# Seven products instead of eight in the down projection of three groups, with weight sums made by adding DMAs

## The chip, the cores and the metric

The kernel runs on one core of a Trainium2 chip. The core has a matrix engine (TensorE, PE in the rows, with its weight loads as PEld), a vector engine (VectorE, DVE), a scalar engine (ScalarE, ACT), GpSimd (POOL) and a queue engine (SyncE, SP) from which most transfers are started. The metric is the device time of one execution in microseconds (us), smaller is better; the time before is the median of three runs.

## The reference

One layer of a decoder trunk on x of 512 tokens by 1024, in float32:

```python
h = rmsnorm(x, g1)
p = h @ w_in                      # attention 6x64, SSD 6 heads, pooling
x = x + concat(moba(p), ssd(p), pool(p)) @ w_out
h2 = rmsnorm(x, norm_ffn)
g, u = h2 @ w_gate, h2 @ w_up     # hidden width 2816
x = x + (silu(g) * u) @ w_down    # 2816 -> 1024
out = rmsnorm(x, norm_final)
```

The change lies in the last matrix product, `(silu(g) * u) @ w_down`, and in the preparation of the gate and up weights.

## The kernel before

**Products.** Every float32 product is made of three matmuls (`mm3`, L188 to L190): each operand is split into a rounded part `hi` (written by ACT, L881) and the rest `lo` (written by DVE, L882), and hi·hi, lo·hi and hi·lo are summed in a PSUM bank (128 x 512 floats). TensorE writes PSUM; DVE and ACT read it.

**The feed-forward part** begins at about 190 us in the trace and ends with the kernel. The hidden width is cut into 22 tiles of 128 (`FT`), in six groups: `GROUPS = ((0,4), (4,8), (8,12), (12,16), (16,18), (18,22))`. For each tile but tile 0 the gate and up projections together are made in seven half-size products (a Strassen form with sums of weights), numbered 1 to 7, each of 12 matmuls with 256 columns, 84 for a tile (`block`). Their results lie in three banks of the tile, psA, psB and psC; `block_out` (L1123 to L1146) copies or adds them to `g`, `ur` and `a`, with one short instruction of ACT or DVE behind each product. The tile's result `a` (128 x 512, silu(g)·u transposed) is split into `aTh` and `aTl`.

**The down projection of a group** comes after its tiles. For each half h of the 1024 output columns, for each tile k and for each of the four token tiles t, three matmuls of 512 columns add into `pd<group><h>_<t>`: 2 x 4 x 4 x 3 = 96 matmuls for a group of four tiles. After a half, four adds (`add_x1`, L814) put the four banks onto the residual `x1`. The weights are split into `dh` and `dl`, 128 x 1024 each, four pairs for a group.

**Preparation of weights.** Every weight tile is loaded from HBM by SP into one of four buffers (`NRAW`): `r_g`, `r_u` and `r_d`, 512 KB each. The `plan` is a list of stages: `split_g`, `add_up` (four adds of 512 columns on DVE, L931 to L934, that form the weight sums `sa` and `sb`), `split_v`, two of `split_s`, and `split_d`. Each stage takes places in a ring of 8 tiles (`w`) or 10 tiles (`wx`), and `done` gives them back when a product has used them. `advance` starts the next stage after each product where the ring has room and the planner's clock says that the load has landed; `need` forces it. The order of the products on TensorE is written by `pair_order`, and a static scheduler then fixes the order of each engine's instructions. Each engine works through its own list in order; an instruction that waits holds up all behind it on that engine.

Of the kernel before, what the change touches and what calls it, by code (L numbers as in the profile page):

```python
# [26 lines left out]
P = 128  # L27
S = 512
# [9 lines left out]
NRAW = 4  # L38
PLAIN = (0,)
# [77 lines left out]
def layer(tc, xT, xn, w1, wz, wv, wo, wgu, wd, par, poolw, gffn, gfin, out):  # L117
# [3 lines left out]
    with ctx:  # L121
# [685 lines left out]
        sp = fpool("sums", 2)  # L807
# [60 lines left out]

        ops = {}
# [14 lines left out]
        def all_loads():  # L884
            for lo_, hi_ in GROUPS:
                order = [(w, i) for i in range(lo_, hi_) for w in "gu"]
                if lo_ == 0:
                    first = [(w, i) for i in PLAIN for w in "gu"] + [("g", i) for i in EARLY]
                    order = first + [q for q in order if q not in first]
                for w, i in order:  # L890
                    yield (w, i), wgu[2 * i + (w == "u")]
                for h in range(2):
                    for kp in range(lo_ // 2, hi_ // 2):
                        yield ("d", kp, h), wd[2 * kp + h]

        loads = all_loads()
# [4 lines left out]

        def load_ahead():
            while len(raws) < NRAW:
                key, src = next(loads, (None, None))
                if key is None:
                    return
                raws[key] = rawp.tile([P, 1024], F32, name="r_" + "_".join(map(str, key)), tag="raw")
                nc.sync.dma_start(raws[key], src)
                dma_free[0] = max(dma_free[0], L.clock) + 1.6
                landed[key] = dma_free[0] + 2.5  # L910
# [6 lines left out]
        sums = {}  # L917

# [7 lines left out]
        def add_up(i):  # L926
            load_ahead()
            r0, r1 = raws["g", i], raws["u", i]
            g1, g2, v1, v2 = r0[:, :512], r0[:, 512:], r1[:, :512], r1[:, 512:]
            s_, q_ = sums[i] = [sp.tile([P, 1024], F32, name=f"{n}{i}", tag="s") for n in ("sa", "sb")]  # L930
# [4 lines left out]
            used(("g", i))  # L935

# [27 lines left out]
        plan = []  # L964
        for gi, (lo_, hi_) in enumerate(GROUPS):
            for i in range(lo_, hi_):
                stages = [("wx", 2, split_g, i), ("w", 0, add_up, i), ("wx", 1, split_v, i), ("wx", 2, split_s, i, 0), ("w", 2, split_s, i, 1)]
                if i in PLAIN:
                    stages = [("wx", 2, split_plain, i, "g"), ("wx", 2, split_plain, i, "u")]
                    if i == PLAIN[-1]:  # L970
                        stages += [("wx", 2, split_g, k) for k in EARLY]
                elif i in EARLY:
                    stages = stages[1:]
                plan += stages
            for h in range(2):
                for kp in range(lo_ // 2, hi_ // 2):
                    plan.append(("w", 2, split_d, kp, h))
# [4 lines left out]
        def advance(must=False):  # L982

            if not plan or live[plan[-1][0]] + plan[-1][1] > cap[plan[-1][0]]:
                return False
            load_ahead()
            _, _, f, *a = plan[-1]
            key = (a[1], a[0]) if f is split_plain else (takes.get(f.__name__), *a)
            if not must and key[0] and L.clock < landed.get(key, 1e9):
# [126 lines left out]
        aT = {}  # L1116
        gf = [None]
# [7 lines left out]
        def block_out(i, n, e):  # L1125
            gl, gr, ur = slice(0, 256), slice(256, 512), slice(256, 512)
            if n in (1, 6, 7):
                u_ = e["u1" if n == 1 else "u2" if n == 6 else "u3"] = (fw if n == 1 else ap_).tile(
                    [P, 256], F32, name=f"u{n}_{i}", tag=f"u{n}", bufs=len(EARLY) + 1 if n == 1 else 2
                )  # L1130
                nc.scalar.copy(u_, e["B"])  # L1131
            elif n == 2:
                e["g"] = fw.tile([P, S], F32, name=f"g{i}", tag="g", bufs=4)
                add(e["g"][:, gl], e["A"], e["u1"])
                nc.scalar.activation(e["g"][:, gl], e["g"][:, gl], AF.Silu)
            elif n == 4:
                e["a"] = e.get("a") or ap_.tile([P, S], F32, name=f"a{i}", tag="a")
                nc.vector.scalar_tensor_tensor(e["a"][:, :256], e["B"], -1.0, e["g"][:, gl], ALU.mult, ALU.mult)
            elif n == 3:
                add(e["g"][:, gr], e["C"], e["u2"])  # L1140
                last = nc.scalar.activation(e["g"][:, gr], e["g"][:, gr], AF.Silu)
                if i == FT - 1:

                    with tc.issue_after(last.ins):
                        nc.scalar.activation(tiny.tile([P, NT], F32, name="pre2", tag="pre"), rstd, AF.Sqrt)
                nc.vector.scalar_tensor_tensor(e["a"][:, ur], e["ur"], -1.0, e["g"][:, gr], ALU.mult, ALU.mult)  # L1146
                out_aT(i, e["a"])
                st.pop(i)
            if n in (5, 7) and "u3" in e and "C" in e:
                e["ur"] = ap_.tile([P, 256], F32, name=f"ur{i}", tag="ur")  # L1150
                add(e["ur"], e["C"], e["u3"])

        def block(i, n):
# [3 lines left out]
            e = st.setdefault(i, {})  # L1157
            which = {1: "B", 6: "B", 7: "B", 4: "B", 2: "A", 5: "C", 3: "C"}[n]
# [46 lines left out]
        def pair_order(lo_, hi_):


            tiles = [i for i in range(lo_, hi_) if i not in PLAIN]
            order = []
            for i, nxt in zip(tiles, tiles[1:] + [None]):  # L1210
                if (i, 6) not in order:
                    order += [(i, n) for n in (1, 2, 6, 5, 7) if (i, n) not in order and (i, n) not in FIRST and (n > 2 or i not in st)]
                if nxt is None and hi_ == 18:

                    return order + [(hi_, 1), (i, 4), (hi_, 2), (i, 3)], []
                if nxt is None:
                    return order, [(i, 4), (i, 3)]
                if nxt in EARLY:
                    order += [(nxt, 6), (i, 4), (nxt, 5), (i, 3), (nxt, 7)]
                else:  # L1220
                    order += [(nxt, 1), (i, 4), (nxt, 2), (i, 3)]

        for gi, (lo_, hi_) in enumerate(GROUPS):
# [91 lines left out]
def pack(inputs):  # L1315
# [23 lines left out]
    wgu = np.ascontiguousarray(wg).reshape(2 * FT, P, 1024)  # L1339
    wdn = f["w_down"][0].reshape(FT // 2, 2, P, 2, 512).transpose(0, 3, 2, 1, 4)  # L1340
# [15 lines left out]
    for g in range(4):  # L1356
# [3 lines left out]
        xT=xT, xn=x.reshape(NT, P, D), w1=w1, wz=wz, wv=wv, wo=wo, wgu=wgu, wd=wdn, par=par, poolw=poolw,  # L1360
# [19 lines left out]
```

## Time and profile before

| | before |
|---|---|
| median of 3 runs | 566.23 us (565.95 to 566.3) |
| profiled execution | 566.83 us, its span 565.0 us, granted clock 0.997 |
| TensorE busy | 555.0 us, 98% of the span |
| VectorE busy | 432.9 us, 77% |
| ScalarE busy | 305.4 us, 54% |
| GpSimd busy | 24.9 us, 4% |
| bytes moved | 61.61 MB, mean 109 GB/s |

The profiled execution is one execution with the hardware profiler on; its span is the time from its first to its last recorded instruction. Busy shares are averages over stages; what bounds a stage is read from that stage alone.

### The profile page before, as it was taken

How to read it: one execution, taken by the hardware profiler on the slowest of the kernel's cores; microseconds unless marked ns; L12 is line 12 of the kernel's file. 1: busy time of each engine (PE TensorE's matmuls, PEld its weight loads, DVE VectorE, ACT ScalarE, POOL GpSimd, SP SyncE). 2: the span in 40 equal slices, each digit the busy share in tenths (PEclk: the TensorE clock that was granted, in tenths of full speed). 3: DMA queues.
4: the chain of work that ended last, by engine and by line, in shares of the span. 5: the costliest groups of instructions: out<-in, count | busy, mean ns of one | idle time of the engine just before them, and what ended most of it. 6: DMA issues, size and time to landing. Idle time of an engine off the chain costs nothing.

```text
span 565.0 us, 9054 instructions
## 1 busy us (share of the span) xinstructions
PE 555.0 (98%) x3500; PEld 502.2 (89%) x3500; DVE 432.9 (77%) x793; ACT 305.4 (54%) x562; POOL 24.9 (4%) x43
## 2 busy tenths in 40 slices
PE   8999999999999999999999999999999999999994
PEld 4998998888978889998899989998999889999984
DVE  5489766898998678999977776876877876876456
ACT  6676635777678447655365525543354525434344
POOL 2020002006110000000000000000000000000000
PEclk9999999999999999999999999999999999999998
DMA  8852232423114501355242232334043333212003
GB/s 279 297 182 76 75 127 98 131 77 103 65 39 148 224 2 37 102 170 177 74 148 93 99 111 75 115 118 142 29 156 83 108 111 113 87 64 75 1 1 148
DMA packets 19807, 61.61 MB, mean 109 GB/s; under 512 B 2333, under 2 KB 4021, under 8 KB 19765
## 3 DMA queue, kind: packets, MB, share of 16 engines
q1 hardware_dynamic: 19188, 60.00, 31.8%
q10 hardware_dynamic: 576, 1.05, 0.5%
q8 instruction: 27, 0.44, 0.3%
q14 instruction: 16, 0.12, 0.1%
HBM read 58.93 MB, written 2.11 MB: 108 GB/s over the span
## 4 chain that ended last, share of the span: by engine, by line
PE 85%; DVE 8%; ACT 2%; DMA 2%; issue 1%; SPq 1%; DVEq 0%; ACTq 0%
PE psB L188 7%; PE psB L190 7%; PE psB L189 7%; PE pd L188 6%; PE pd L189 6%; PE pd L190 6%; PE pc L188 4%; PE pc L190 4%; PE pc L189 4%; PE psC L190 3%; PE psC L189 3%; PE psC L188 3%; PE po L188 2%; PE po L189 2%; PE po L190 2%; PE pn L188 2%
## 5 line engine op out<-in xcount | busy, mean ns | idle before, releaser
L189 PE MATMUL pd<-dl,aTh 128*128 128x512 f32 x160 | 62.4, 390 | 0.0
L188 PE MATMUL pd<-dh,aTh 128*128 128x512 f32 x160 | 61.4, 391 | 0.0
L190 PE MATMUL pd<-dh,aTl 128*128 128x512 f32 x160 | 59.1, 390 | 0.0
L158 DVE TENSOR_TENSOR wlo<-raw,whi 128x1024 fp32r<-128x1024 f32 (+4 forms) x35 | 37.2, 1066 | 12.7 <-ACT whi L157 12.7
L157 ACT ACTIVATE whi<-raw 128x1024 fp32r<-128x1024 f32 (+4 forms) x36 | 32.0, 892 | 21.2 <-PE pc L189 11.5
L881 ACT ACTIVATE sh<-sb 128x1024 fp32r<-128x1024 f32 x21 | 22.3, 1060 | 36.9 <-PE pd L189 15.5
L1131 ACT COPY u<-psB 128x256 f32<-128x256 f32 x63 | 23.2, 368 | 34.7 <-PE psB L190 34.0
L188 PE MATMUL pc<-hT_hi,whi 128*128 128x512 f32 x104 | 41.7, 401 | 0.0
L190 PE MATMUL pc<-hT_hi,wlo 128*128 128x512 f32 x104 | 40.8, 392 | 0.0
L189 PE MATMUL pc<-hT_lo,whi 128*128 128x512 f32 x104 | 40.7, 391 | 0.0
L882 DVE TENSOR_TENSOR gl<-r_g,gh 128x1024 fp32r<-128x1024 f32 x22 | 26.9, 1224 | 15.1 <-ACT gh L881 10.6
L881 ACT ACTIVATE dh<-r_d 128x1024 fp32r<-128x1024 f32 x22 | 23.3, 1058 | 24.0 <-PE psC L189 11.6
L881 ACT ACTIVATE gh<-r_g 128x1024 fp32r<-128x1024 f32 x22 | 23.3, 1058 | 23.0 <-DMA r_g<-wgu 12.8
L188 PEld LDWEIGHTS pd<-dh,aTh 128*128 128x128 f32 x160 | 30.0, 188 | 6.2 <-ACT aTh L881 0.4
L190 PEld LDWEIGHTS pd<-dh,aTl 128*128 128x128 f32 x160 | 29.9, 188 | 6.1
L189 PEld LDWEIGHTS pd<-dl,aTh 128*128 128x128 f32 x160 | 30.1, 188 | 5.8
L814 DVE TENSOR_TENSOR x<-pd,x 128x512 f32<-128x512 f32 x44 | 27.9, 686 | 8.1 <-PE pd L190 8.1
L882 DVE TENSOR_TENSOR sl<-sa,sh 128x1024 fp32r<-128x1024 f32 x21 | 25.7, 1224 | 8.8 <-PE psA L189 8.2
L882 DVE TENSOR_TENSOR sl<-sb,sh 128x1024 fp32r<-128x1024 f32 x21 | 25.6, 1221 | 8.0 <-ACT sh L881 8.0
L881 ACT ACTIVATE sh<-sa 128x1024 fp32r<-128x1024 f32 x21 | 22.3, 1062 | 14.6 <-DVE sa L932 9.0
L882 DVE TENSOR_TENSOR dl<-r_d,dh 128x1024 fp32r<-128x1024 f32 x22 | 26.9, 1222 | 4.1 <-ACT dh L881 4.0
L188 PE MATMUL po<-whi,mixT_hi 128*128 128x512 f32 x64 | 25.4, 400 | 0.0
(322 smaller groups left out, 1827.1 us busy)
## 6 DMA issues: line engine op xcount, KB each, us to landing
r_g<-wgu SPq DMA_DIRECT2D x22, 512.0 KB, 3.3
r_u<-wgu SPq DMA_DIRECT2D x22, 512.0 KB, 3.6
r_d<-wd SPq DMA_DIRECT2D x22, 512.0 KB, 3.4
raw<-w SPq DMA_DIRECT2D x13, 512.0 KB, 3.3
raw<-wo SPq DMA_DIRECT2D x8, 512.0 KB, 3.2
rawn<-xn SPq DMA_DIRECT2D x4, 512.0 KB, 5.8
x<-xn SPq DMA_DIRECT2D x4, 512.0 KB, 7.3
raw<-wz SPq DMA_DIRECT2D x4, 390.0 KB, 3.8
```

Of the source, the lines that this page charges most:

```text
L157: high = nc.scalar.activation(hi[:, sl], raw[:, sl], AF.Copy)
L158: eng.tensor_tensor(lo[:, sl], raw[:, sl], hi[:, sl].bitcast(F32), ALU.subtract)
L188: nc.tensor.matmul(ps, s_hi, m_hi, start=first, stop=False, skip_group_check=chain)
L189: nc.tensor.matmul(ps, s_hi, m_lo, start=False, stop=False, skip_group_check=chain)
L190: last_mm = nc.tensor.matmul(ps, s_lo, m_hi, start=False, stop=last, skip_group_check=chain)
L814: nc.vector.tensor_tensor(x1[t][:, cs], ps, x1[t][:, cs], ALU.add)
L881: high[name] = nc.scalar.activation(hi, src, AF.Copy).ins
L882: eng.tensor_tensor(lo, src, hi.bitcast(F32), ALU.subtract)
L1131: nc.scalar.copy(u_, e["B"])
```

## The change

For groups 1, 2 and 3 (`FAST`, tiles 4 to 15) the down projection is made in seven products in place of eight. The group's four tiles are two pairs `kp`; of each pair the 256 hidden rows by 512 tokens are one operand, cut into 2 x 2 blocks, and the weight (256 by 1024) the other. Seven sums of weight blocks R1 to R7 (`split_r`, 128 x 1024 with both pairs side by side) are multiplied with seven sums of blocks of `a` (`out_fast`, parts a1 to a7). One step (`down_step`) is one product for one pair: two token tiles of three matmuls of 512 columns, 6 matmuls. Seven products for two pairs make 84 matmuls for a group. Products 1, 6, 7, 4 chain in the banks `dnB0` and `dnB1`, products 2, 3, 5 in `dnA0` and `dnA1`; after the second pair of each product two adds put its banks onto `x1`: 14 adds for a group.

The steps don't stand behind the group: `MERGED` writes them between the products of the next group's first two tiles (n0, n1) and the last two products of the group's last tile (nl).

From tile 4 on (`ADD_FROM`) two of a tile's four weight sums are made by transfers: SP loads one array into a buffer, and a second transfer, started by GpSimd, adds another array to it (`sum_ahead`). The same forms two of the seven R. The new input `wgs` holds copies of blocks of `wgu` in another order. The up weights' load is half as large from there on. Buffers change: three for sums in place of two (one sum `R7` of a group lies in the buffer of `gn`), three in place of four for `u1` and for `g`. From tile 4 on, product 5 goes into the second half of psA's bank, and `ur` lies in the second half of psB's bank.

```diff
+FAST = (1, 2, 3)
+MERGED = (
+    "n0.1 1a nl.4 n0.2 1b nl.3 2a n0.5 6a n0.6 2b n0.7 6b n1.1 n0.4 5a n1.2 5b n0.3 7a n1.5 7b n1.6 3a n1.7 3b 4a 4b"
+).split()
...
-        sp = fpool("sums", 2)
+        sp = fpool("sums", SUM_BUFS)
...
+                    for sl, src in wd_block(key[1], *first):
+                        nc.sync.dma_start(t_[:, sl], src)
+                    for sl, src in wd_block(key[1], *second):
+                        nc.gpsimd.dma_start(t_[:, sl], src, accum_op=ALU.add)
+                else:
+                    nc.sync.dma_start(t_, wgs[2 * key[0]])
+                    nc.gpsimd.dma_start(t_, wgs[2 * key[0] + 1], accum_op=ALU.add)
...
+            if i >= ADD_FROM:
+
+                nc.vector.tensor_tensor(g1, sums[i, 0][:, :512], g1, ALU.add)
+                nc.vector.tensor_tensor(g2, g1, g2, ALU.add)
...
+        def split_r(kp, n):
+            load_ahead()
+            h_, l_ = (slot(R_RING[n - 1], f"r{x_}{kp}_{n}") for x_ in "hl")
...
+            if n == 6:
+
+                nc.vector.tensor_tensor(raws[r00], sums["r", kp, 5], raws[r00], ALU.add)
+                nc.vector.tensor_tensor(raws[r10], raws[r00], raws[r10], ALU.add)
...
-                e[which] = bank(f"ps{which}_{i}")[:, :256]
+                if which == "C" and i >= ADD_FROM:
+                    b_ = e["ac"][:, 256:]
...
-                e["ur"] = ap_.tile([P, 256], F32, name=f"ur{i}", tag="ur")
+                e["ur"] = e["bank"][:, 256:]
...
+        def out_fast(i, a_):
...
+            if j == 0:
+                half[kp] = a_
+                aT[1, kp] = part("a1", a_[:, L_])
+                nc.vector.tensor_tensor(a_[:, L_], a_[:, L_], a_[:, R_], ALU.subtract)
+                aT[5, kp] = part("a5", a_[:, L_], q)
+                return
+            a0 = half.pop(kp)
+            h_, l_ = part("a2", a_)
...
+            nc.vector.tensor_tensor(a0[:, R_], a_[:, R_], a0[:, R_], ALU.subtract)
+            sub(a_[:, R_], a0[:, L_], a_[:, R_])
+            sub(a_[:, L_], a_[:, R_], a_[:, L_])
+            h_, l_ = part("a4", a_)
...
+            aT[7, kp] = part("a7", a0[:, R_], q + 1)
...
+        def down_step(_, gi, n, c):
...
+            a_hi, a_lo = aT[n, kp0 + c]
+            new = n in (1, 2, 5)
+            for v in range(2):
+                vs = slice(v * P, (v + 1) * P)
+                mm3(ps[v], a_hi[:, vs], a_lo[:, vs], w_hi[:, js], w_lo[:, js], new and c == 0, c == 1, chain=not new)
+            if c:
...
+                    t0, h, op = {1: (0, 0, 0), 2: (0, 0, 0), 6: (2, 0, 0), 3: (2, 0, 0), 7: (2, 1, 1), 5: (2, 1, 1), 4: (0, 1, 1)}[n]
+                    cs = slice(h * 512, (h + 1) * 512)
+                    for v in range(2):
+                        x_ = x1[t0 + v][:, cs]
+                        if op:
+                            nc.vector.tensor_tensor(x_, x_, ps[v], ALU.subtract)
+                        else:
+                            add(x_, ps[v], x_)
```

TensorE at the start of group 1's down projection, before: psB_7 is the last product of tile 7, `pd10_0` and `pd10_1` are the first two token tiles of the group's half 0, `dh20` and `aTh4` the split weights and the split result of tile 4.

```order
L188 MATMUL psB_7_3437<-T3h_2329,sh17_3359 128x256
L189 MATMUL psB_7_3437<-T3l_2330,sh17_3359 128x256
L190 MATMUL psB_7_3437<-T3h_2329,sl17_3360 128x256
L188 MATMUL pd10_0_3550<-dh20_3382,aTh4_3246 128x512
L189 MATMUL pd10_0_3550<-dl20_3383,aTh4_3246 128x512
L190 MATMUL pd10_0_3550<-dh20_3382,aTl4_3247 128x512
L188 MATMUL pd10_1_3551<-dh20_3382,aTh4_3246 128x512
L189 MATMUL pd10_1_3551<-dl20_3383,aTh4_3246 128x512
L190 MATMUL pd10_1_3551<-dh20_3382,aTl4_3247 128x512
```

The same place after: psB_8 is product 1 of the next group's tile 8, `dnB0` and `dnB1` the two banks of step 1a, with `rh2_1` (R1) and the part `a1` of pair 2.

```order
L199 MATMUL psB_8_3580<-h2_hi_2077,gh8_3400 128x256
L200 MATMUL psB_8_3580<-h2_lo_2078,gh8_3400 128x256
L201 MATMUL psB_8_3580<-h2_hi_2077,gl8_3401 128x256
L199 MATMUL dnB0_1_3603<-rh2_1_3445,a1h2_3254 128x512
L200 MATMUL dnB0_1_3603<-rl2_1_3446,a1h2_3254 128x512
L201 MATMUL dnB0_1_3603<-rh2_1_3445,a1l2_3255 128x512
L199 MATMUL dnB1_1_3604<-rh2_1_3445,a1h2_3254 128x512
L200 MATMUL dnB1_1_3604<-rl2_1_3446,a1h2_3254 128x512
L201 MATMUL dnB1_1_3604<-rh2_1_3445,a1l2_3255 128x512
L199 MATMUL psA_8_3636<-h2_hi_2077,gh8_3400 128x256
L200 MATMUL psA_8_3636<-h2_lo_2078,gh8_3400 128x256
L201 MATMUL psA_8_3636<-h2_hi_2077,gl8_3401 128x256
```

Eight runs of 96 matmuls are now steps of 6 between products of 12; the down projection no longer stands in one piece, and its first matmuls come while tiles 8 and 9 are being made.

DVE at the same stage before: four of the group's eight adds from `pd10_0` to `pd10_3` and the first from half 1 (`pd11_0`), among the weight sums of tiles 9 and 10.

```order
L882 TENSOR_TENSOR aTl7_3596<-a7_3578,aTh7_3595 128x512
L931 TENSOR_TENSOR sa10_3800<-r_u_10_3644 128x512
L932 TENSOR_TENSOR sa10_3800<-sa10_3800,r_g_10_3627 128x512
L882 TENSOR_TENSOR sl19_3708<-sb9_3673,sh19_3707 128x1024
L814 TENSOR_TENSOR x1_0_2052<-pd10_0_3550,x1_0_2052 128x512
L814 TENSOR_TENSOR x1_1_2053<-pd10_1_3551,x1_1_2053 128x512
L814 TENSOR_TENSOR x1_2_2054<-pd10_2_3552,x1_2_2054 128x512
L933 TENSOR_TENSOR sb10_3801<-r_g_10_3627,r_u_10_3644 128x512
L934 TENSOR_TENSOR sb10_3801<-sa10_3800,r_g_10_3627 128x512
L814 TENSOR_TENSOR x1_3_2055<-pd10_3_3553,x1_3_2055 128x512
L814 TENSOR_TENSOR x1_0_2052<-pd11_0_3691,x1_0_2052 128x512
```

And after: `rl2_5` and `rl2_7` are the `lo` parts of R5 and R7, `sar_2_5` and `sar_2_7` their sums by transfer, `sa9_0` the sum by transfer of tile 9, `x1_0<-dnB0` the add behind step 1b, `h2_lo<-a6` the `lo` of part a7 or a5.

```order
L927 TENSOR_TENSOR gl9_3633<-r_g_9_3551,gh9_3632 128x1024
L1267 TENSOR_TENSOR psB_7_3449<-psA_7_3484,u7_7_3565 128x256
L1375 TENSOR_TENSOR a6_3480<-a6_3480 128x256
L927 TENSOR_TENSOR rl2_5_3653<-sar_2_5_3211,rh2_5_3652 128x1024
L1001 TENSOR_TENSOR r_g_9_3551<-sa9_0_3347,r_g_9_3551 128x512
L1267 TENSOR_TENSOR x1_0_2052<-dnB0_1_3603,x1_0_2052 128x512
L1267 TENSOR_TENSOR x1_1_2053<-dnB1_1_3604,x1_1_2053 128x512
L927 TENSOR_TENSOR rl2_7_3668<-sar_2_7_3090,rh2_7_3667 128x1024
L927 TENSOR_TENSOR h2_lo_2078<-a6_3480,h2_hi_2077 128x256
L1002 TENSOR_TENSOR r_g_9_3551<-r_g_9_3551 128x512
L1282 SCALAR_TENSOR_TENSOR a7_3630<-psB_7_3449,g7_3497 128x256
L927 TENSOR_TENSOR vh9_3749<-r_u_9_3601,vh9_3749 128x512
```

An add into `r_g_9` from a sum by transfer (`sa9_0`) now stands directly ahead of the adds onto `x1`, and splits of R stand among them.

GpSimd's list before ends its work with the attention part and has nothing in the feed-forward part:

```order
L720 MEMSET pwb1_1706 128x16
L502 TENSOR_TENSOR sz_227<-skp_242,sz_227 128x384 x2
L158 TENSOR_TENSOR wlo30_2097<-raw30_2095,whi30_2096 128x512
L1376 UNCONDITIONAL_BRANCH
L1376 ISA
```

After, adding transfers stand behind the same work, 24 rows to the end of the kernel (`sar` rows are two transfers each):

```order
L169 TENSOR_TENSOR wlo30_2097<-raw30_2095,whi30_2096 128x512
L983 DMA sar_2_7_3090<-wd 128x512 x2
L986 DMA sa4_0_2722<-wgs 128x1024
L986 DMA sa5_0_2773<-wgs 128x1024
L986 DMA sa6_0_2795<-wgs 128x1024
L986 DMA sa7_0_3029<-wgs 128x1024
L986 DMA sa8_0_3078<-wgs 128x1024
L983 DMA sar_2_5_3211<-wd 128x512 x2
```

GpSimd's transfers come in one list, in the order in which the sums are wanted.

## Rows read from the trace of the kernel before

**Rows 1.** The page, part 1: busy time and share of the span.
```profile
PE 555.0 (98%) x3500; PEld 502.2 (89%) x3500; DVE 432.9 (77%) x793; ACT 305.4 (54%) x562; POOL 24.9 (4%) x43
```

**Rows 2.** The page, part 4: the chain that ended last, by engine.
```profile
PE 85%; DVE 8%; ACT 2%; DMA 2%; issue 1%; SPq 1%; DVEq 0%; ACTq 0%
```

**Rows 3.** Windows by stage: start:end, length, busy time by engine, clock, DMA share, GB/s.
```profile
241.00:280.00 39.00, 39.00 (x239) 35.00 (x239) 36.92 (x55) 19.39 (x27) 0.00 (x0) 1.00 0.44 144
331.90:394.00 62.10, 62.10 (x433) 58.31 (x432) 45.89 (x68) 28.24 (x45) 0.00 (x0) 1.00 0.31 102
394.00:456.10 62.10, 62.10 (x433) 58.31 (x433) 44.56 (x67) 27.90 (x45) 0.00 (x0) 1.00 0.31 103
490.00:546.00 56.00, 56.00 (x390) 52.26 (x390) 32.21 (x52) 21.09 (x36) 0.00 (x0) 1.00 0.11 38
```

**Rows 4.** Timeline of TensorE where group 1's down projection starts: start, duration, instruction.
```profile
313.74 0.28 PE L188 MATMUL psB<-T3h,sh 128*128 128x256 f32 x1
...
315.18 0.40 PE L188 MATMUL pd<-dh,aTh 128*128 128x512 f32 x1
...
319.97 0.39 PE L188 MATMUL pd<-dh,aTh 128*128 128x512 f32 x1
```

**Rows 5.** Timeline of DVE, instructions back to back.
```profile
384.52 1.22 DVE L882 TENSOR_TENSOR sl<-sa,sh 128x1024 fp32r<-128x1024 f32 x1
385.65 1.22 DVE L882 TENSOR_TENSOR dl<-r_d,dh 128x1024 fp32r<-128x1024 f32 x1
386.78 0.42 DVE L1123 TENSOR_TENSOR g<-psC,u 128x256 f32<-128x256 f32 x1
387.12 1.22 DVE L882 TENSOR_TENSOR sl<-sb,sh 128x1024 fp32r<-128x1024 f32 x1
388.25 0.42 DVE L1146 SCALAR_TENSOR_TENSOR a<-ur,g 128x256 f32<-128x256 f32 x1
388.58 0.69 DVE L933 TENSOR_TENSOR sb<-r_g,r_u 128x512 f32<-128x512 f32 x1
389.19 0.69 DVE L934 TENSOR_TENSOR sb<-sa,r_g 128x512 f32<-128x512 f32 x1
389.79 0.69 DVE L882 TENSOR_TENSOR aTl<-a,aTh 128x512 fp32r<-128x512 f32 x1
```

**Rows 6.** Lines by form, 280 to 565 us: ACT's and DVE's own kinds, mean ns.
```profile
L881 ACT ACTIVATE dh<-r_d 128x1024 fp32r<-128x1024 f32 x18 | 19.1, 1059 | 19.3 <-PE psC L189 11.6 <-PE pd L189 7.1 <-ACT g L1135 0.5
L881 ACT ACTIVATE aTh<-a 128x512 fp32r<-128x512 f32 x18 | 11.3, 631 | 7.8 <-DVE a L1146 7.8
L1135 ACT ACTIVATE g<-g 128x256 f32<-128x256 f32 x18 | 7.4, 410 | 4.5 <-DVE g L1123 4.4
L814 DVE TENSOR_TENSOR x<-pd,x 128x512 f32<-128x512 f32 x38 | 24.3, 686 | 7.3 <-PE pd L190 7.3
```

**Rows 7.** The page, part 6: DMA issues, KB each, median us from issue to landing.
```profile
r_g<-wgu SPq DMA_DIRECT2D x22, 512.0 KB, 3.3
r_u<-wgu SPq DMA_DIRECT2D x22, 512.0 KB, 3.6
x<-xn SPq DMA_DIRECT2D x4, 512.0 KB, 7.3
```

**Rows 8.** The page, part 2: shares in 40 slices of the span, in tenths; GB/s.
```profile
POOL 2020002006110000000000000000000000000000
DMA  8852232423114501355242232334043333212003
GB/s 279 297 182 76 75 127 98 131 77 103 65 39 148 224 2 37 102 170 177 74 148 93 99 111 75 115 118 142 29 156 83 108 111 113 87 64 75 1 1 148
```

**Rows 9.** Waits, 241 to 546 us: engine, line, releaser, us, times, longest.
```profile
ACT gh L881 <- DMA r_g<-wgu: 12.2, 6, 3.3
...
DVE sa L931 <- DMA r_u<-wgu: 8.2, 5, 3.4
...
DVE x L814 <- PE pd L190: 6.4, 4, 4.7
```

More of the change, by code (lines that the diff above doesn't have):

```diff
@@ L882, in hi_lo, with wd_block, source @@
             eng.tensor_tensor(lo, src, hi.bitcast(F32), ALU.subtract)
[L884 to L896, printed above, removed]
+        def wd_block(kp, j, h):
+            return [(slice(c * 512, (c + 1) * 512), wd[2 * (kp + c) + h][:, j * 512 : (j + 1) * 512]) for c in range(2)]
+        def source(key):
+            if key[0] == "d":
+                return [(slice(0, 1024), wd[2 * key[1] + key[2]])]
+            if key[0] == "r":
+                return wd_block(*key[1:])
+            w, i = key
+            half = 512 * (w == "u" and i >= ADD_FROM)
+            return [(slice(half, 1024), wgu[2 * i + (w == "u")][:, half:])]
+        loads = []
         raws = {}
@@ L900, in layer, with lands @@
         takes = {"split_g": "g", "add_up": "u", "split_v": "u", "split_d": "d"}
+        def lands(key, busy, wait):
+            lag = LAG if L.clock > LAG_FROM else 0.0
+            dma_free[0] = max(dma_free[0], L.clock + lag) + busy
+            landed[key] = dma_free[0] + wait
         def load_ahead():
             while len(raws) < NRAW:
-                key, src = next(loads, (None, None))
-                if key is None:
+                if not loads:
                     return
+                key = loads.pop(0)
                 raws[key] = rawp.tile([P, 1024], F32, name="r_" + "_".join(map(str, key)), tag="raw")
-                nc.sync.dma_start(raws[key], src)
-                dma_free[0] = max(dma_free[0], L.clock) + 1.6
-                landed[key] = dma_free[0] + 2.5
+                for sl, src in source(key):
+                    nc.sync.dma_start(raws[key][:, sl], src)
+                lands(key, 1.6, 2.5)
         def used(*keys):
@@ L935, in add_up @@
             used(("g", i))
+            if i == ADD_FROM - 1:
+                sum_ahead()
         def split_v(i):
@@ L978, in layer @@
+        for _, _, f, *a in plan:
+            for key in inputs(f, a):
+                if key[0] != "s" and key not in loads:
+                    loads.append(key)
+                elif key[0] == "s" and key[1:] not in to_add and key[-1] != (OWN_SUM if key[1] == "r" else None):
+                    to_add.append(key[1:])
         plan = plan[::-1]
@@ L987, in advance @@
             _, _, f, *a = plan[-1]
-            key = (a[1], a[0]) if f is split_plain else (takes.get(f.__name__), *a)
-            if not must and key[0] and L.clock < landed.get(key, 1e9):
+            if not must and any(L.clock < landed.get(key, 1e9) for key in inputs(f, a)):
                 return False
@@ L1157, in block @@
             e = st.setdefault(i, {})
+            did.add((i, n))
             which = {1: "B", 6: "B", 7: "B", 4: "B", 2: "A", 5: "C", 3: "C"}[n]
@@ L1160, in block @@
             if new:
-                e[which] = bank(f"ps{which}_{i}")[:, :256]
+                if which == "C" and i >= ADD_FROM:
+                    b_ = e["ac"][:, 256:]
+                else:
+                    b_ = bank(f"ps{which}_{i}")
+                e[which] = b_[:, :256]
+                if which == "A" and i >= ADD_FROM:
+                    e["ac"] = b_
+                if which == "B":
+                    e["bank"] = b_
             ps = e[which]
@@ L1200, in out_aT @@
         def out_aT(i, a_):
-            h_, l_ = (ap_.tile([P, S], F32R, name=f"aT{x_}{i}", tag=f"aT{x_}", bufs=NA) for x_ in "hl")
+            if any(GROUPS[g][0] <= i < GROUPS[g][1] for g in FAST):
+                return out_fast(i, a_)
+            h_, l_ = (ap_.tile([P, S], F32R, name=f"aT{x_}{i}", tag=f"aT{x_}512", bufs=NA) for x_ in "hl")
             hi_lo(a_, h_, l_, nc.vector)
             aT[i] = (h_, l_)
[L1205 to L1221, printed above, removed]
```

177 lines of the change are left out of this document (150 added, 27 removed).

## Prediction

> **What bounds the kernel now.** I read the page's busy shares first. TensorE is busy for 98% of the span, DVE for 77%, ACT for 54%, GpSimd for 4% [rows 1], and TensorE carries 85% of the chain that ended last [rows 2]. Those are means, so next come windows by stage. Groups 2 and 3 each take 62.10 us, and in each TensorE is busy for all 62.10 us at full granted clock (1.00), while DVE works 44.6 to 45.9 us (72 to 74%), ACT 28 us, and the DMA engines 31% at 102 to 103 GB/s [rows 3]. From 241 to 280 us and from 490 to 546 us it is the same: TensorE's busy time equals the window. So in the feed-forward part nothing but TensorE's list sets the time; loads, splits and adds end in time. What a removed matmul gives is its distance to the next one in the pipeline, and not its listed duration. The timeline shows this distance: from 313.74 to 315.18 us stand 12 products of 256 columns, 0.120 us each; from 315.18 to 319.97 us stand 21 matmuls of 512 columns, 0.228 us each [rows 4], though they are listed with 0.28 and 0.40 us.
>
> **What is removed: matmuls.** A group of four tiles has 4 x 84 = 336 matmuls of 256 columns, 336 x 0.120 = 40.3 us, so its 96 down matmuls take 62.10 - 40.3 = 21.8 us, 0.227 us each, which agrees with the timeline. Seven products need 84. Twelve fewer are 12 x 0.227 = 2.72 us for a group, 59.4 us in place of 62.1, and 8.17 us for the three groups. The matmuls that stay have the same shapes, so I keep their distance, also where 256 and 512 columns alternate.
>
> **What is added on DVE.** Back to back, an instruction of 128x1024 takes 1.13 us (384.52 to 385.65), of 512 columns 0.60, of 256 columns 0.34 [rows 5]. For one group go: 4 `aTl` (2.4 us), 4 `dl` (4.5), 8 adds onto x1 (4.8), and 8 of 16 adds for weight sums (4.8): 16.5 us. There come: 4 `lo` parts of 512 columns for a2, a3, a4, a6 (2.4), 6 `lo` parts and 8 block sums of 256 columns (14 x 0.34 = 4.8), 7 `lo` of R (7.9), 2 sums of R in place (2.3), 14 adds onto x1 (8.4): 25.8 us. Net 9.3 us, so DVE works 44.6 + 9.3 = 53.9 us of 59.4, 91%. In the merged stretch it is denser: TensorE has 84 x 0.227 + 168 x 0.120 = 39.2 us there; DVE has two tiles' own work, 2 x (44.6 - 16.5) / 4 = 14.0 us, and the 25.8 us but for the parts of the first pair (3.6): 36.2 us, 92%. The best comparison in the trace is the window 241 to 280 us, where DVE is 95% busy (36.92 of 39.00) and TensorE never stops [rows 3]. So I cost DVE's work at nothing; TensorE's 39.2 us hides it. If that cover is gone, each microsecond over 39.2 costs one.
>
> **On ACT.** The `hi` parts: 7 of 1024, 4 of 512 and 6 of 256 columns (7.4 + 2.5 + 2.5 us) in place of 4 and 4 (4.2 + 2.5) by [rows 6]; 27.9 + 5.6 = 33.5 us of 59.4. Nothing.
>
> **The transfers.** A group now loads 4 gate tiles (0.524 MB each), 4 half up tiles, 3 tiles of `w_down` and six pairs of a load and an adding transfer: 2.1 + 1.05 + 1.57 + 6.3 = 11.0 MB in 59.4 us, 185 GB/s, against 6.3 MB now. At the share per byte of today (0.31 at 102 GB/s) the plain loads take 40% of the DMA engines' time; the adds take 16% at a load's price and 32% if an addend costs double. The sum, 56 to 73%, is below the first two slices of the span, where the engines carried 279 and 297 GB/s at 80% [rows 8]. The single wait matters more than the share. No transfer that adds, and none from GpSimd's list, is in this trace, and GpSimd has done nothing since the middle of the span [rows 8]. A plain 512 KB load lands 3.3 us after its issue; the slowest 512 KB row is 7.3 us [rows 7]. I bound the adding transfer by 3.3 us below and by twice 7.3, 14.6 us, above, so a pair takes 6.6 to 17.9 us; I take about 8, nearer to the loads of the same stage. Against that stands the lead. Five of a group's six pairs go through three buffers, one each 59.4 / 5 = 11.9 us; a buffer is free at the latest one such interval after its pair was wanted, and then two intervals, 23.8 us, are left to refill it. Both ends of the bound fit, and I cost the pairs at nothing.
>
> A page speaks against this: the Trainium skill, Collectives: The Full Stack, in its section on the bandwidth ceiling, says of a summing transfer that "the add needs two source reads" and so runs at half the rate of a copy. By that a pair would be 3.3 + 6.6 = 9.9 us (estimate) and the sum the same, since 9.9 is under 23.8; no run here shows it yet.
>
> **New waits.** Each is weighed by TensorE's work between cause and use. (1) Step 6a adds into the banks that step 1b leaves to two DVE adds: 39 matmuls of 256 and 3 of 512 columns lie between, 5.4 us, against 2 x 0.60 plus 0.40 for the last matmul's end. What stands ahead of the adds on DVE (an add into `r_g`, a split of R) may take 1.7 us more. (2) From tile 4 on product 5 lies in psA's bank and waits until DVE has added product 2 from there: 24 matmuls, 2.9 us, against 0.28 + 0.42. (3) ACT's copy of a psB result before the next chained product: the shortest gap that I count is three 512-column matmuls (0.68 us), in tile 18, against 0.28 for the matmul's end and 0.37 for the copy. Nothing is lost by these rows. I allow 0.1 us for each merged stretch, 0.3 in all; from below 0, from above rival B.
>
> **Sum.** The profiled execution: 566.83 - 8.17 + 0.3 = 558.96 us. It lies 0.60 above the median of 566.23, so the median goes to **558.4 us**, 1.4% faster. The start, the attention part, group 0 and groups 4 and 5 keep TensorE's matmuls; there the adding transfers only lighten DVE (two adds fewer a tile), which is not the bound.
>
> **Rivals.**
>
> *B, part of it is given back to DVE.* 92% is a mean; DVE's list is in order, and a stage that comes early (a split waiting for ACT) or an `a` part that waits for its tile leaves holes that the remaining 8%, 3.0 us a stretch, must hold. If holes eat more, the adds behind steps 1b, 2b, 6b and product 5's bank come late, and TensorE stops. For it: even now DVE waits 6.4 us for the last pd matmul and 8.2 us for `r_u` [rows 9]. Against it: 95% from 241 to 280 us. At 1 to 2 us a group the time is 558.1 + 3 to 6: 561 to 564 us. The shared banks matter for this case: the Trainium skill, PSUM — Partial Sum Buffer, under bank collisions, wants the guard by bank and not by address, so product 5 has to wait for DVE although its columns are others. By the rows that wait costs something only when DVE is over 2.2 us late (2.9 - 0.70).
>
> *C, slower: the adding transfers come late.* `r_g<-sa` stands on DVE directly ahead of the adds onto x1. If a pair takes longer than 23.8 us, DVE waits there, and behind it wait the evacuations that free TensorE's banks. A group then takes 5/3 x (pair + 11.9) us. It equals 62.1 at a pair of 25.4 us, from which point the change loses; at 27 us a group takes 64.8 and the kernel 566.2 + 3 x 2.7 = 574 us. For it: GpSimd's transfers are one list whose order holds back later ones, the loads ahead of them on SP wait for the same buffers and hold the gate loads behind them, and ACT waits for `r_g` already, six times, at most 3.3 us [rows 9]. Around the change from group 0 to group 1, where the DMA share is 44% before anything is added [rows 3], it is likeliest. Against it: it needs eight times a load's landing.
>
> *D, no gain.* The merged stretches lose as much as they save, 2.7 us each, by B's holes or by C's delays of a pair around 25 us: 565 to 567.3 us.
>
> **How the numbers follow.** The forecast A gets 0.63 (557.5 to 560.5 us), B 0.16, C 0.16, D 0.05. About 0.2%, 1.1 us, is what a measurement of this kernel tells from no change. A and B are faster: 0.79; D is the same: 0.05; C is slower: 0.16. The range takes in A and B and leaves out C and D: 557.3 to 564.5 us; its low end is the full 8.2 us and 0.8 more for a slightly shorter distance in the mixed stretches.
>
> **What the profile after would show.** Right: windows of groups 1 to 3 that add up to 8.2 us less, TensorE's busy time equal to the window, 36 matmuls fewer at the same 0.12 and 0.227 us; DVE near 90% there; 24 transfers from GpSimd landing in 4 to 15 us; in DVE's waits no large row for them. B would show as TensorE idle before `psB`, `ps` of product 5 or `dnB` matmuls, released by DVE, with DVE free of DMA waits. C would show as DVE idle before `r_g<-sa` or ACT before `rh<-sar`, released by a transfer. I am wrong in the sum if a 512-column matmul between 256-column ones takes longer than 0.227 us: 252 x 0.01 us would be 2.5 us.

## The result and the profile after

The changed kernel takes **559.68 us** (median of 4 runs, 558.78 to 560.42), the kernel before 566.21 us in the same place: ratio 0.9885, 95% interval 0.9866 to 0.9904. That is 6.5 us less, where 7.8 were forecast. The profiled execution is the slowest of the four: 560.42 us, span 558.7.

The page after, parts 1, 3 (queue, packets, MB, share of the 16 DMA engines) and 6:

```profile
PE 546.7 (98%) x3464; PEld 495.1 (89%) x3464; DVE 450.8 (81%) x832; ACT 316.3 (57%) x589; POOL 51.2 (9%) x73
...
q1 hardware_dynamic: 24372, 66.29, 35.4%
q0 software_dynamic: 4320, 12.58, 13.4%
...
r_g<-wgu SPq DMA_DIRECT2D x22, 512.0 KB, 4.3
sa<-wgs SPq DMA_DIRECT2D x18, 512.0 KB, 4.5
sa<-wgs POOLq DMA_DIRECT2D x18, 512.0 KB, 6.7
```

Windows after (columns as in [rows 3]): the change from group 0 to 1, and the stretch of group 3's tiles (12 to 15) with group 2's steps from 1b on and group 3's step 1a.

```profile
250.00:262.00 12.00, 12.00 (x71) 10.59 (x70) 8.04 (x14) 7.25 (x11) 1.75 (x2) 1.00 0.95 266
382.00:441.00 59.00, 59.00 (x418) 55.48 (x417) 53.69 (x86) 32.59 (x54) 7.00 (x8) 1.00 0.74 192
```

From 382 to 441 us the forecast's picture stands: TensorE never idles at full granted clock, DVE works 91%, ACT 55%, the DMA engines 74% at 192 GB/s. The other row is what the forecast had not reckoned: 95% DMA share, where the kernel before has 55% in the same 12 us:

```profile
250.00:262.00 12.00, 12.00 (x76) 10.83 (x76) 10.81 (x17) 6.92 (x9) 0.00 (x0) 1.00 0.55 175
```

TensorE's only listed wait between 241 and 484 us lies just behind this window:

```profile
PE pd L199 <- DVE g L1267: 1.5, 1, 1.5
```

The chain of waits from 240 to 275 us tells where it is from (start, length, what):

```profile
247.89 1.14 DVE dl L927
249.05 7.71 DMA r_g<-wgu
256.78 1.07 ACT gh L926
257.87 0.83 DVE gl L927
...
260.63 0.61 DVE vh L927
261.26 4.36 DMA r_u<-wgu
265.70 0.64 ACT vh L926
266.40 0.57 issue
266.98 0.42 DVE a L1282
267.39 1.15 DVE sl L927
268.55 0.60 DVE r_g L1001
269.15 0.34 DVE g L1267
269.54 0.50 PE pd L199
```

Tile 4's gate load takes 7.71 us (a plain load took 3.3 in [rows 7]). Tile 4's split is late by it, so the buffer of tile 4's up load is given back late, and tile 5's up load starts late, at 261.26. Tile 5's split `vh` waits for that one, and behind it in DVE's list stands `g<-psC` of tile 3, which frees the bank that group 0's next down matmul writes. In starts: the matmul before lies at 267.67, the next at 269.54, 1.64 us over the usual 0.23.

### The profile page after: what moved, and what is told of

Its sections match the earlier page's. It is cut to its first block, busy times and chain, and to the rows that moved or that the text cites. A ratio compares the mean times of both kernels' runs of the same rounds, so it can differ in the third digit from the quotient of the medians.

```text
span 558.7 us, 9204 instructions
## 1 busy us (share of the span) xinstructions
PE 546.7 (98%) x3464; PEld 495.1 (89%) x3464; DVE 450.8 (81%) x832; ACT 316.3 (57%) x589; POOL 51.2 (9%) x73
## 3 DMA queue, kind: packets, MB, share of 16 engines
q1 hardware_dynamic: 24372, 66.29, 35.4%
q0 software_dynamic: 4320, 12.58, 13.4%
## 4 chain that ended last, share of the span: by engine, by line
PE 80%; DVE 11%; DMA 4%; ACT 2%; issue 1%; SPq 1%; DVEq 0%; ACTq 0%
PE psB L201 6%; PE psB L200 6%; PE psB L199 6%; PE psA L201 5%; PE psA L200 5%; PE psA L199 5%; PE pc L199 4%; PE pc L201 4%; PE pc L200 4%; PE po L199 2%; PE po L200 2%; PE po L201 2%; PE pn L199 2%; PE pn L200 2%; PE pn L201 2%; PE dnB L199 2%
## 5 line engine op out<-in xcount | busy, mean ns | idle before, releaser
L986 POOL DMA_DIRECT2D sa<-wgs x18 | 15.6, 869 | 184.9 <-DMA sa<-wgs 49.4
L926 ACT ACTIVATE sh<-r_g 128x1024 fp32r<-128x1024 f32 x18 | 19.0, 1057 | 15.8 <-PE psA L200 6.4
L199 PE MATMUL pd<-dh,aTh 128*128 128x512 f32 x64 | 24.8, 395 | 1.7 <-DVE g L1267 1.5
L200 PE MATMUL po<-wlo,mixT_hi 128*128 128x512 f32 x64 | 25.0, 390 | 0.0
L201 PE MATMUL psB<-T2h,sl 128*128 128x256 f32 x84 | 24.0, 285 | 0.9 <-DVE sl L927 0.9
L200 PE MATMUL pd<-dl,aTh 128*128 128x512 f32 x64 | 24.7, 392 | 0.0
L927 DVE TENSOR_TENSOR sl<-r_g,sh 128x1024 fp32r<-128x1024 f32 x18 | 21.9, 1218 | 3.1 <-ACT sh L926 3.1
L199 PE MATMUL psB<-T2h,sh 128*128 128x256 f32 x84 | 23.8, 284 | 0.0
L199 PE MATMUL psB<-h_hi,gh 128*128 128x256 f32 x84 | 23.8, 284 | 0.0
L200 PE MATMUL psA<-h_lo,gh 128*128 128x256 f32 x84 | 23.8, 283 | 0.0
```

Source lines behind the costliest of these rows:

```text
L199: nc.tensor.matmul(ps, s_hi, m_hi, start=first, stop=False, skip_group_check=chain)
L200: nc.tensor.matmul(ps, s_hi, m_lo, start=False, stop=False, skip_group_check=chain)
L201: last_mm = nc.tensor.matmul(ps, s_lo, m_hi, start=False, stop=last, skip_group_check=chain)
L926: high[name] = nc.scalar.activation(hi, src, AF.Copy).ins
L927: eng.tensor_tensor(lo, src, hi.bitcast(F32), ALU.subtract)
L986: nc.gpsimd.dma_start(t_, wgs[2 * key[0] + 1], accum_op=ALU.add)
```

## The experiments

Four things could explain the missing 1.3 us: late loads at that one place (L), DVE's load in the merged stretches (D, the prediction's rival B), the distance of the matmuls, and the changed buffers.

**The changed kernel again, and its transfers moved.** `again` is the changed kernel without an edit. `late_third` loads tile 6's sum behind tile 4's gate and up loads, `late_two` the sums of tiles 5 and 6; `add8` starts the sums by transfer at tile 8.

```diff
 # late_third, late_two: LATE = (6,) or (5, 6); sum_ahead() for these is called in split_v(4)
-                    nc.sync.dma_start(t_, wgs[2 * key[0]])
+                    if key[0] in LATE:
+                        with tc.issue_after(load_ins["u", ADD_FROM]):
+                            nc.sync.dma_start(t_, wgs[2 * key[0]])
+                    else:
+                        nc.sync.dma_start(t_, wgs[2 * key[0]])
 # add8
-ADD_FROM = 4
+ADD_FROM = 8
```

> The changed kernel unchanged, to see its spread. Theory L (late loads): in the profiled execution the three merged stretches ran without a stall and the 36 matmuls gave their 8.2 us; what is missing, about 1.7 us, was lost once, in group 0's second half of the down projection, where the gate load of tile 4 took 7.71 us because three transfers of tile sums stood ahead of it. Such a lateness differs from run to run, so L expects executions in two bands, near 558.9 and near 560.4 us, and in the profile either a TensorE gap of about 1.6 us near 269 us or none. Theory D (DVE): the missing time lies in the merged stretches, a little in each, and executions scatter evenly with gaps before dnB or psA matmuls.

> One move: the plain load of tile 6's sum is issued behind the gate and up loads of tile 4, no longer ahead of them. L expects the gate load of tile 4 to land in 4 to 6 us in place of 7.71, the gap in group 0's down projection to fall from 1.6 us to under 0.5, and 558.4 to 559.2 us with less spread. D expects no change, 559 to 560.4 us.

> The sums of tiles 5 and 6 are both loaded behind the gate and up loads of tile 4. L expects the gate load of tile 4 to land in 3.3 to 5 us and the gap gone, 558.2 to 558.8 us, unless tile 5's sum is now the late one: it is wanted some 10 us later, and a pair took 8 to 14 us there. D expects no change, 559 to 560.4 us.

> Sums by transfer only from tile 8 on: tiles 4 to 7 have their four adds on DVE as before, so no adding transfer of a tile runs between 241 and 280 us, and DVE has 4.8 us more in group 1. L expects no gap in group 0's down projection and 558.2 to 558.9 us. D expects DVE's 4.8 us to cost in group 1: 560 to 563 us.

Measured, beside a kernel before of 566.09 us:

| run | median us (range, runs) | ratio to before | TensorE's wait in group 0's down projection, us | group 0, us | behind it, us |
|---|---|---|---|---|---|
| again | 560.79 (559.03 to 564.65, 6) | 0.9912 (0.9887 to 0.9936) | 2.7 | 72.89 | 261.55 |
| late_third | 560.25 (559.84 to 564.44, 6) | 0.9916 (0.9889 to 0.9942) | 0.3 | 67.65 | 261.59 |
| late_two | 560.31 (559.62 to 561.15, 4) | 0.9896 (0.9882 to 0.9909) | 0.9 | 68.25 | 261.55 |
| add8 | 559.72 (559.34 to 560.53, 4) | 0.9887 (0.9874 to 0.9900) | none | 67.35 | 261.83 |

The last three columns are from one profiled execution each, the last two from TensorE's starts: from the first gate product to tile 4's first product, and from there to the last part of the down projection. The first profile after has 68.84 and 261.58 us, the kernel before 66.49 and 268.98. So behind group 0 these five profiles agree within 0.3 us, and what they lose differently lies in group 0. With no adding transfer near, the wait is gone: L holds for the place. Windows of `add8` over the same time show why, 55% DMA share in place of 95%:

```profile
250.00:262.00 12.00, 12.00 (x68) 10.51 (x67) 11.04 (x18) 7.81 (x11) 0.00 (x0) 1.00 0.55 176
```

The two reorderings only shrink the wait, and their medians can't be told from `again`. Tile 4's gate load still takes 6.71 us in `late_third`, where L expected 4 to 6, and in `late_two` the chain runs through the adding transfer of a sum, 7.94 us. The two bands that L expected are no bands: `again` scatters over 5.6 us. In its slowest execution, the profiled one, tile 4's gate load takes 7.61 us, much as in the first profile, but tile 5's up load 5.72 in place of 4.36, and it shows what a longer wait does. TensorE's timeline in it:

```profile
267.88 0.39 PE L201 MATMUL pd<-dh,aTl 128*128 128x512 f32 x1
271.01 0.79 PE L199 MATMUL pd<-dh,aTh 128*128 128x512 f32 x1 [2.74 <-DVE g L1267]
271.60 0.63 PE L200 MATMUL pd<-dl,aTh 128*128 128x512 f32 x1
272.02 0.63 PE L201 MATMUL pd<-dh,aTl 128*128 128x512 f32 x1
```

And its window behind the gap (columns as in [rows 3]):

```profile
271.00:277.00 6.00, 5.99 (x14) 4.74 (x15) 2.71 (x4) 1.03 (x2) 0.32 (x1) 0.50 0.86 254
```

Behind the gap the granted clock is 0.50, its lower level of 1.2 GHz, and a matmul starts every 0.43 us in place of 0.23 until about 277 us. Fourteen matmuls at 0.20 more cost another 2.9 us: the wait is paid twice. Behind the 1.64 us of the first profile the clock stayed at 1.00. All four medians are 1.4 to 2.5 us above 558.3 (566.09 less the 7.8 that were forecast), though, which L's numbers had not allowed for, and the median of `add8`, without the wait, is no lower than the 559.68 of the first measurement. So the wait is shown in the profiles, and not in the medians. What `add8` still lacks stands in its starts too: 0.9 us more than before in group 0, in short waits of `psB` matmuls, and 7.2 us saved behind it in place of 8.2.

**More work for DVE.** One or two instructions of 512 columns more behind each product's two adds, on the base of `add8` (the values don't change):

```diff
 # dve1; dve2 has range(2)
+                    for _ in range(1):
+                        nc.vector.tensor_tensor(x_, x_, x_, ALU.max)
```

> As the run with sums by transfer from tile 8 on, with one more DVE instruction of 512 columns behind the two adds of each product (the maximum of x1 with itself): 7 x 0.60 = 4.2 us more a group, 58.1 of 59.4 us in groups 2 and 3 and more than the whole 59.4 in group 1. If a DVE below its mean limit costs nothing, groups 2 and 3 lose under 0.5 us each and group 1 some 3 us: 562 to 564 us. If the holes in its list already count (the rival of a part given back), groups 2 and 3 lose 1.5 to 3 us each: 565 to 569 us. If DVE had no part in it at all: 559.7.

> The same with two such instructions behind each product, 8.4 us more a group: 62.3 us of DVE's work in 59.4 in groups 2 and 3, 67.1 in group 1. DVE as the bound gives 2.9 + 2.9 + 7.7 us over 559.7, 573 us; with holes in its list besides, up to 582 us; no part of DVE in it, 559.7.

Measured: 560.94 us (ratio 0.9903, 0.9890 to 0.9917) with one, 571.61 (1.0083, 1.0057 to 1.0108) with two; `add8` had 0.9887. So 4.2 us more for DVE in each group cost about 0.9 us in all three together, by the ratios, and 8.4 us more cost 11 us. The first lies below every band that had DVE count, and 1.2 us above the time without it. DVE in the changed kernel has room for several microseconds a group, and D falls: it is not where the 1.3 us went. With one more instruction DVE works 95% from 324 to 382 us and 96% from 382 to 441:

```profile
324.00:382.00 58.00, 57.54 (x412) 54.11 (x410) 55.09 (x88) 29.83 (x51) 7.00 (x8) 1.00 0.73 192
382.00:441.00 59.00, 59.00 (x420) 55.61 (x420) 56.41 (x90) 32.60 (x54) 7.03 (x8) 1.00 0.65 171
```

**The steps written together** (also on the base of `add8`):

```diff
-    "n0.1 1a nl.4 n0.2 1b nl.3 2a n0.5 6a n0.6 2b n0.7 6b n1.1 n0.4 5a n1.2 5b n0.3 7a n1.5 7b n1.6 3a n1.7 3b 4a 4b"
+    "n0.1 nl.4 n0.2 nl.3 1a 1b 2a 6a 2b 6b 5a 5b 7a 7b 3a 3b 4a 4b n0.5 n0.6 n0.7 n1.1 n0.4 n1.2 n0.3 n1.5 n1.6 n1.7"
```

> As the run with sums by transfer from tile 8 on; the seven products' steps of a group are written one behind the other, before the rest of the next tiles' products, and not alternating with them. If the alternation is what hides DVE's 22 us for the steps, TensorE's gaps of 0.5 us and more appear before dnA and dnB matmuls in each of the three groups, 2 to 4 us a group, and the time is 565 to 572 us. If DVE has room enough anyway, the time is the same or up to 0.4 us lower, since fewer matmuls of 512 columns follow one of 256 (0.028 us lost at each such change).

Measured: 580.84 us (ratio 1.026, 1.022 to 1.030), worse than expected. TensorE's waits from 280 to 500 us:

```profile
PE psB L199 <- DVE g L1267: 7.2, 2, 4.8
PE dnA L199 <- ACT a2h L926: 2.1, 1, 2.1
PE psB L199 <- ACT sh L926: 1.7, 3, 0.9
PE psA L199 <- DVE g L1267: 0.4, 1, 0.4
```

The matmuls and DVE's instructions are as many as in `add8`; only the order differs (the splits are planned from the same list and move with it), and it is worth 21 us. The listed waits are 11.4 us of it, most of them for DVE's `g`; from 390 to 420 us the mean granted clock is 0.89. So the order is what makes DVE's 22 us for the steps free. The alternation has a price of its own, below the resolution of the waits' view. TensorE after, where a piece of 16 matmuls stands between products (the rest of the piece left out):

```profile
341.89 0.28 PE L199 MATMUL psA<-T1h,sh 128*128 128x256 f32 x1
342.01 0.40 PE L199 MATMUL dnB<-rh,a4h 128*128 128x512 f32 x1
342.24 0.40 PE L200 MATMUL dnB<-rl,a4h 128*128 128x512 f32 x1
...
342.94 0.39 PE L199 MATMUL dnA<-rh,h_hi 128*128 128x512 f32 x1
...
345.67 0.28 PE L200 MATMUL psA<-T1l,sh 128*128 128x256 f32 x1
345.78 0.28 PE L201 MATMUL psA<-T1h,sl 128*128 128x256 f32 x1
```

The first four take 0.233 us each, the twelve behind them 0.2275. The order shows 41 pieces of 2 to 18 matmuls in the three groups; put together from the starts, the 252 matmuls take 58.0 us, 0.2303 each, where 0.2269 would be 57.2: 0.9 us. That is not the whole account: behind a piece the next matmul of 256 columns often starts after 0.11 us in place of 0.12 (the last two lines). Whole groups give the price with this counted in, from the first matmul of step 1a in groups 1, 2 and 3:

```profile
312.36 0.40 PE L199 MATMUL dnB<-rh,a1h 128*128 128x512 f32 x1
...
371.84 0.40 PE L199 MATMUL dnB<-rh,a1h 128*128 128x512 f32 x1
...
431.36 0.40 PE L199 MATMUL dnB<-rh,a1h 128*128 128x512 f32 x1
```

A group takes 59.48 and 59.52 us, where 62.10 - 2.72 = 59.38 were forecast: 0.12 us a group, **0.4 us** in the three.

**Without the seven products, and the buffers alone.** `FAST = ()` with the sums by transfer from tile 4 or 8 on, and the kernel before with the changed kernel's buffers:

```diff
 # fast0; add8_fast0 has ADD_FROM = 8 besides
-FAST = (1, 2, 3)
+FAST = ()
 # before_sums3, in the kernel before
-        sp = fpool("sums", 2)
+        sp = fpool("sums", 3)
-                    [P, 256], F32, name=f"u{n}_{i}", tag=f"u{n}", bufs=len(EARLY) + 1 if n == 1 else 2
+                    [P, 256], F32, name=f"u{n}_{i}", tag=f"u{n}", bufs={1: 3, 6: 2, 7: 1}[n]
...
-                e["g"] = fw.tile([P, S], F32, name=f"g{i}", tag="g", bufs=4)
+                e["g"] = fw.tile([P, S], F32, name=f"g{i}", tag="g", bufs=3)
```

> No group in seven products (all down projections as before), with the sums by transfer from tile 4 on and the changed buffers. Theory L: the matmuls are as many as before, and what the changed kernel lost outside the products stays: some 0.5 us in group 0 by the order of the sums, 1 to 3 us by late loads between groups 0 and 1: 567 to 569.5 us. If the transfers of sums had no price: 566.2 to 566.8.

> The same with sums by transfer from tile 8 on, so none runs between groups 0 and 1. L expects no gap there and 566.4 to 567.2 us; its distance to the run with seven products and sums from tile 8 on (559.7 us) is then 7 us, the 36 matmuls' 8.2 us less about 1 us for the 512-column matmuls that follow 256-column ones (0.230 us each in place of 0.227). If the seven products gave their full 8.2 us, 568.0.

> The kernel before with the changed kernel's buffers alone: three sums, three u1, three g. If the third buffer lets the first add of tile 2's sums move ahead of the split that TensorE waits for, the gap of 0.6 us near 234 us shows here too and the time is 566.4 to 567.0 us. If buffers have no part in it: 566.2 and no such gap.

Measured, beside 566.17 us: 571.19 (1.0092, 1.0062 to 1.0122), 570.20 (1.0060, 1.0039 to 1.0082) and 568.59 us (1.0038, 1.0027 to 1.0050). All three are slower than expected. The buffers alone cost 2.4 us in this order. About 0.6 us of it, by the starts, is the order that the expectation named: DVE of `before_sums3`, where the add `sa<-r_u` of tile 2 has moved ahead of the split `sl` of tile 1's sum,

```profile
231.84 0.68 DVE L934 TENSOR_TENSOR sb<-sa,r_g 128x512 f32<-128x512 f32 x1
232.44 0.68 DVE L931 TENSOR_TENSOR sa<-r_u 128x512 f32<-128x512 f32 x1
233.04 1.22 DVE L882 TENSOR_TENSOR sl<-sa,sh 128x1024 fp32r<-128x1024 f32 x1
```

and TensorE's waits in this run, where the largest, for `aTh`, stands at 254 us in group 0's down projection:

```profile
PE pd L188 <- ACT aTh L881: 1.1, 1, 1.1
PE psB L190 <- DVE sl L882: 0.9, 2, 0.5
PE psB L188 <- DVE x L814: 0.2, 1, 0.2
```

In the kernel before the only listed wait is 0.2 us; the changed kernel has the same 0.9 us for `sl`. In the `fast0` profile the same wait for `g<-psC` as after stands again (2.1 us): it belongs to the transfers, not to the products. Between `add8_fast0` and `add8` lie 10 us, more than the matmuls of the seven products: by the starts some 2 us are gaps of `add8_fast0` at 308 to 324, 448 and 489 us that `add8` does not have. The waits' view lists one of them, 0.6 us for `dl`; what ends the others is not shown.

**An order changed.** For tiles 2 and 3, the first add of a tile's sums is held behind the split of the one before, on the base of `add8`:

```diff
+            if i in (2, 3):
+                with tc.issue_after(low[i - 1, 0]):
+                    nc.vector.tensor_tensor(s_[:, :512], v1, v2, ALU.add)
...
```

> As the run with sums by transfer from tile 8 on, and one order more: the first add of the sums of tiles 2 and 3 comes behind the split of the sum of the tile before, as in the kernel before the change. With three sum buffers that add (0.60 us) had moved ahead of the split for which TensorE waits; TensorE's gap at 234 us was 0.64 us against 0.04 before. Theory L (what is missing was lost in group 0 and at the change of matmul sizes, not in the merged stretches) expects that gap to fall below 0.15 us and 0.5 us less than the run without this order, 559.0 to 559.4 us. Theory D (DVE's load in the merged stretches) expects no difference.

Measured: 564.10 us (0.9957, 0.9944 to 0.9971), 4.4 us slower than `add8`. The gap at 234 us is gone, but TensorE now waits for `sl` at 236 and 239 us, 1.2 us together in place of 0.9: the expected gain is not there. The static scheduler reordered what follows too, in the last groups as well, where TensorE now waits 2.8 us for `aTh` and the granted clock falls again, to a mean of 0.61 in the window behind it:

```profile
541.10:545.50 4.40, 4.39 (x12) 3.50 (x13) 1.59 (x3) 0.18 (x1) 0.00 (x0) 0.61 0.01 4
```

So the 0.5 us could not be won this way.

**The adding transfers doubled:**

```diff
                     nc.gpsimd.dma_start(t_, wgs[2 * key[0] + 1], accum_op=ALU.add)
+                    nc.gpsimd.dma_start(t_, wgs[2 * key[0] + 1], accum_op=ALU.add)
```

> The changed kernel; every adding transfer of a tile is made twice (so the second addend counts twice in two of the four weight sums of tiles 4 to 21). A pair takes some 17 us in place of 11 and the DMA engines have 20% more work in groups 1 to 3, about 0.95 of their time. The rival of late adding transfers expects DVE to wait in front of the adds into the gate tiles in every group, TensorE's gaps over 2 us with the granted clock falling to half behind them: 570 to 585 us. If a lead of 24 us hides 17, only the stretch between groups 0 and 1 gets worse: 562 to 566 us.

Measured: 572.58 us (1.0097, 1.0071 to 1.0123), at the low end of the rival's 570 to 585. But its mechanism stands in one place only, not in every group. The stretch from group 0 to 1 is filled: DVE waits 5.1 us there for a sum in front of a gate tile, TensorE 4.7 us behind it, and the granted clock is 0.50 from 273 to 276 us. The next groups lose one wait of 1.6 to 1.8 us each in two of them. Its windows:

```profile
241.00:283.00 42.00, 37.26 (x212) 32.79 (x211) 27.50 (x40) 18.05 (x25) 7.80 (x9) 0.92 1.00 261
324.00:382.00 58.00, 56.40 (x394) 52.69 (x394) 51.23 (x82) 31.47 (x53) 10.54 (x12) 1.00 0.87 212
```

At a DMA share of 0.87 the lead hid most of it, at 1.00 it did not.

## Why the prediction was right

**The matmuls: right.** 36 fewer at 0.227 us are 8.17 us; three runs of 96 are now three times 84, in 41 pieces. From the first gate product to the last part of the down projection the profiled executions differ by 335.5 - 330.4 = 5.0 us. TensorE's timeline before, the first `pspg` matmul, tile 4's first product and the first `pdl` matmul:

```profile
211.26 0.28 PE L188 MATMUL pspg<-h_hi,gh 128*128 128x256 f32 x1
...
277.75 0.28 PE L188 MATMUL psB<-h_hi,gh 128*128 128x256 f32 x1
...
546.73 0.39 PE L188 MATMUL pdl<-dh,aTh 128*128 128x512 f32 x1
```

The same three after:

```profile
210.41 0.28 PE L199 MATMUL pspg<-h_hi,gh 128*128 128x256 f32 x1
...
279.25 0.28 PE L199 MATMUL psB<-h_hi,gh 128*128 128x256 f32 x1
...
540.83 0.39 PE L199 MATMUL pdl<-dh,aTh 128*128 128x512 f32 x1
```

Up to tile 4's first product the changed kernel takes 2.35 us more, behind it 7.40 less. The 2.35 us are 1.7 for the wait behind tile 4's late load and 0.6 for short waits of `psB` matmuls, by the starts, where before had some too. Of the 8.17 us, 0.8 are missing behind it: 0.3 by a wait for `aTh` at the end of group 5, 0.4 by the distance, and 0.1 that no row places. The 1.3 us outside (0.9 ahead, 0.4 behind) I don't put down to the change: the start lay between 210.3 and 211.6 us in all profiles, and the tail wasn't tested. So the mechanism of the gain is the one forecast, but that the profiled 560.42 us lies only 1.5 above the sum's 558.96, with 3.1 us missing inside, is in part luck.

**The distance: a term left out.** "The matmuls that stay have the same shapes, so I keep their distance, also where 256 and 512 columns alternate" was a step that failed in size; the prediction named it as a way to be wrong and priced it at 2.5 us for 0.01 us a matmul. The matmuls of the pieces take 0.0034 us more each, 0.9 us, of which about half comes back in the 256-column matmuls behind: 0.4 us are lost.

**DVE and ACT: right.** 53.7 of 59 us against 53.9 of 59.4, ACT 32.6 against 33.5. No matmul of the merged stretches waited, so the allowance of 0.3 us for them was not needed, and rival B falls with `add8_dve1`. Rival C's sign, DVE in front of `r_g<-sa` or ACT in front of `rh<-sar` waiting for a transfer, stands in no row from 241 to 545 us.

**The transfers: right in the groups, wrong between groups 0 and 1.** The load of the groups (74% at 192 GB/s) lies just above the upper end of the forecast (73%), because an addend costs double: 13.4% for 12.58 MB is 1.07% for each MB, and 35.4% for 66.29 MB is 0.53%. All adding transfers come from GpSimd's queue and no plain one does, so no run parts the price of the adding from that of the queue. The Trainium skill, Collectives: The Full Stack, under the bandwidth ceiling, gives a reduce-scatter half the rate of a copy because its add needs two source reads. The ratio of 2.0 here agrees. A pair of landings takes 4.5 + 6.7 = 11.2 us, not 8, and fits its lead. But the argument went by lead and mean share alone, and of group 0 the sum says that there "the adding transfers only lighten DVE". That step failed: they cost 1.7 us there in the first profile and 5.8 in `again`. Where three sums are begun at once the engines are full (95%), and what comes late is the gate load behind them, and not the sums; in `late_two` and `add_twice` it is a sum. Rival C named the place and the mechanism, DVE's list held by a late transfer in front of what frees TensorE's banks, and put it at 24 us of a pair; it took a 7.7 us load. That transfers of GpSimd's list and SP's share the engines is also what the Trainium skill, DMA: Bandwidth & Descriptors, says under issuing engines. The 7.71 us beside 3.2 in `add8` agrees.

**The buffers: wrong.** They were costed at nothing: the prediction asked whether a sum's buffer is refilled in time, and not what their number does to the order. Alone they cost 2.4 us in the old order, and about half a microsecond, in group 0's waits for `sl`, remains in the new one.

## What to carry to other kernels

A product saved on a full TensorE is worth its distance to the next, if another engine's work for it is spread between other products; here the same work in another order cost 21 us. Check DMA by the stretch in which new transfers start, not by their mean and their own lead: here an ordinary load behind them came late. A third buffer isn't free either where a static scheduler uses it to move an instruction ahead of one that the busiest engine waits for.

## What I had not expected of the hardware

A TensorE wait of 2.7 us was followed by about 6 us of half granted clock (0.50) and so cost 5.8 us in all; one of 1.5 us, and one of 2.1 us in `fast0`, were followed by none. Matmuls of 512 columns start 0.233 us apart just behind one of 256 columns and 0.2275 us later in a piece.

What stays open: whether the scatter of the changed kernel, some 5 us where the kernel before stays within about 2, is all in the one wait whose length was seen to differ (1.5 and 2.7 us; behind group 0 its two profiles agree within 0.1 us), and how much of the doubled price of an addend is the adding.
